# Where the block sums of w_down are taken: GpSimd or VectorE, one set behind each column tile of the output projection

## The chip, the cores and the metric

The kernel is one program on one core of a Trainium2 chip. The metric is the device time of one execution in microseconds; of several executions the median is given. The engines are named as the profile names them: PE (TensorE: matmuls and their weight loads), DVE (VectorE), ACT (ScalarE), POOL (GpSimd) and SP (SyncE, which here only issues DMAs). Each engine works its own queue in order; a semaphore holds an instruction, and all that stand behind it on that engine, until what it needs is there.

## The reference, cut to what matters

One decoder layer on 1032 tokens (1024 of a prompt, 8 of samples), width 1024, all float32:

```
proj = rmsnorm(x, norm1_w) @ w_in                       # SSD heads, gate and pooling inputs
y    = concat(ssd_heads(proj), pooled_groups(proj))     # 2048 columns: 12 tiles SSD, 4 tiles pooled
x    = x + y @ w_out                                    # the output projection
u    = causal_dwconv(rmsnorm(x, norm2_w) @ w_up)        # 2 x 2816 columns
gate, val = split(u, 2)
x    = x + (silu(gate) * val) @ w_down                  # 2816 -> 1024
out  = rmsnorm(x, final_norm_w)                         # and the new states
```

## The kernel before

Activations lie transposed: 128 channels on the partitions, 1032 tokens along a row. Every matmul is made of three in a faster number format, with each operand split in a high and a low part (`mm3`, L159 to L161: high by high, high by low, low by high). The high part is a copy on ACT, the low part a subtraction on DVE: L140 and L141 for weights (`raw` from memory to `wop`), L210 and L211 for activations.

The last matmul, by `w_down`, is done as a 2 by 2 block product with seven products in place of eight. Four of the seven (p5, p6, p7, p3) use sums of blocks of `w_down` as weights. These sums do not depend on any activation, so they are made long before they are used, beside the output projection, and stored to memory (`sd` tensors), from where the down phase loads them from 1126.7 us on (L1288).

The output projection (`w_out`, L907 on) runs over K in three passes: `part(ops, 0, 0)` with the first 6 SSD tiles, `part(ops, 6, 1)` with the other 6, and `w_out_end` with the 4 pooled tiles. Below, A0 to A7 are the 8 column tiles of the first pass and B0 to B7 those of the second. A tile is 3 chunks of 344 tokens with 18 matmuls each. For each tile SP loads two pieces of weights of 128x384 (four `raw` buffers: two tiles ahead), ACT and DVE split them (four `wop` buffers, so the pieces of tile n+2 are split when tile n has left theirs), PE multiplies, and DVE adds each chunk's bank to the residual `x` (the evacuation, L920). Four PSUM banks (tag `g`) take turns, so a chunk's bank is wanted again when three more chunks have run. The eighth tile of each pass runs its three chunks together (`gemm_k`).

Before the second pass, the six operands y of that pass are split (`yh` on ACT, `yl` on DVE, L210 and L211); the first of them was split early, the five others stand on the queues behind the last tile's weights.

There are twelve sets of sums, each one a pair (m, s) of a column block and a K piece. In the first pass sets 1 to 6 are made at tiles A0 to A5, in the second sets 7 to 12 at B1 to B6 (`first <= n < first + 6`). A set loads four blocks from `w_down` (`blk` "21" and "22" into one buffer, "11" and "12" into another), 256 KB each in sets 1 to 8 and 192 KB in the others, makes four sums (p5 = 21+22 into the place of 22, p7 = 11-21 into 21, p6 = 22-11 into a third buffer, p3 = 12-p6 into 12), and issues a store of each from POOL. The buffers are those that the pooling stage has left: the pair 11/12 has two buffers of the tag `v`, the pair 21/22 alternates between two tags, and so does the third. So the loads of a set wait until the stores of the set before last have landed. The loads stand on SP's queue among those of `w_out`.

A scheduler that replays the program in its own model of time sets the final order of each engine's queue; `issue_after` (here `self.behind`) keeps an instruction from being placed before another one.

Of the kernel before, what the change touches and what calls it, by code (L numbers as in the profile page):

```python
# [13 lines left out]
ALU = mybir.AluOpType  # L14
# [61 lines left out]
class Kernel:  # L76
# [817 lines left out]
    def w_out(self, pf):  # L894
        nc, d = self.nc, self.d
        ops = []
        for i in range(6):
            o = (self.bigt(F32R, TOK, "yh"), self.bigt(F32R, TOK, "yl"))
            self.split(self.xs[i][:, :TOK], *o)
            ops.append(o)  # L900
        self.x2 = []
        for n in range(KT):
            t = self.bigt(F32, TOK, "x2")
            nc.sync.dma_start(t, d["xT"][:, n])
            self.x2.append(t)

        self.sums = {}  # L907
        todo = [(m, s) for s in range(len(PIECES)) for m in range(KT // 2)]

        def part(ops, k0, first, done=None):  # L910
            for n in range(KT):
                if first <= n < first + 6:
                    self.down_sums(len(todo), *todo.pop(0))
                nk = len(ops)
                ws = self.load_tile(d["wout"][n][:, k0 * P : (k0 + nk) * P], nk, 3 if nk == 6 else 4)
                t = self.x2[n]

                def evac(c, ps):
                    tc_ = t[:, c * CH : (c + 1) * CH]
                    nc.vector.tensor_tensor(out=tc_, in0=tc_, in1=ps, op=ALU.add)  # L920

                (self.gemm_k if n == KT - 1 else self.gemm)(ws, ops, evac)
                if done is not None:
                    done(n)

        part(ops, 0, 0)
        ops = []
        for i in range(6, 12):
            o = (self.bigt(F32R, TOK, "yh"), self.bigt(F32R, TOK, "yl"))
            self.split(self.xs[i][:, :TOK], *o)  # L930
            ops.append(o)
        part(ops, 6, 1)
        ops = []
        for g in range(4):
            o = (self.bigt(F32R, TOK, "ph"), self.bigt(F32R, TOK, "pl"))
            self.split(pf[g], *o)
            ops.append(o)
        self.x2d = self.dram.tile([KT, P, TOK], F32, name="x2d")
        self.w_out_end(ops, 0)

        half = KT // 2
        self.ops = {p: [] for p in CHAIN}

        def beside(n):
            if n == 0:
                return
            for k in {1: (0, 1), 2: (2, 3), 5: (4, 5), 6: (6, 7)}.get(n, ()):
                self.scale(k, 0)
            for k in {3: (0, 1), 4: (2, 3), 6: (4, 5), 7: (6, 7)}.get(n, ()):
                t = self.op_tile()  # L950
                self.split(self.x2[k][:, :TH], t[:, 0], t[:, 1])
                self.ops["p1" if k < half else "p2"].append((t[:, 0], t[:, 1]))

        self.w_out_end(ops, 1, beside)
# [284 lines left out]

    def down_sums(self, i, m, s):  # L1240

        nc, d = self.nc, self.d
        k0, nk = PIECES[s]
        w = nk * P
        mk = lambda tag, bufs=1: self.ph.tile([P, 2, 512], F32, tag=tag, name=self.nm("ds"), bufs=bufs)
        x, y, z = mk("v", 2), mk(("mh", "ml")[i % 2]), mk(("sa", "sb")[i % 2])
        blk = {"11": x[:, 0, :w], "12": x[:, 1, :w], "21": y[:, 0, :w], "22": y[:, 1, :w]}
        for k, r, e in (("21", 1, 0), ("22", 1, 1), ("11", 0, 0), ("12", 0, 1)):
            o = (e * DK + k0) * P
            nc.sync.dma_start(blk[k], d["wdn"][2 * m + r][:, o : o + w])  # L1250

        def mix(p, out, in0, in1, op):
            nc.gpsimd.tensor_tensor(out=out, in0=in0, in1=in1, op=op)
            self.sums[p, m, s] = self.dram.tile([P, w], F32, name=self.nm("sd"))
            nc.gpsimd.dma_start(self.sums[p, m, s], out)

        s2 = z[:, 0, :w]
        mix("p5", blk["22"], blk["21"], blk["22"], ALU.add)
        mix("p7", blk["21"], blk["11"], blk["21"], ALU.subtract)
        mix("p6", s2, blk["22"], blk["11"], ALU.subtract)  # L1260
        mix("p3", blk["12"], blk["12"], s2, ALU.subtract)

    def down_ops(self, p, first=0, end=DK):

# [348 lines left out]
```

## Time and profile before

| what | value |
|---|---|
| median of 3 runs | 1409.85 us (1405.99 to 1411.67) |
| the profiled execution | 1407.76 us, span 1406.0 us |
| busy over the span | PE 97%, DVE 70%, ACT 50%, POOL 40% |
| PE clock granted, mean | 0.984 |
| DMA moved | 228.09 MB, 162 GB/s |
| the sums' stretch (L1250 to L1255) | first loads 507.0 us, first sum 533.5 us, last store issued 651.4 us |

The profile is one execution on the hardware. Times in it are microseconds from the start of the span. A busy PE is not yet a PE at its peak: matmuls overlap, and the granted clock is a column of its own (1.00 is full speed). A row of groups reads: line, engine, operation, out<-in, count, busy time and mean, then the idle time ahead of the group and what ended it. A row of the timeline reads: start, length, engine, line and operation, and in brackets the idle time ahead of it with its releaser. A row of waits reads: who waited for whom, total time, times, longest.

### The profile page before, as it was taken

To read this page: it belongs to the slowest core of one execution; us is meant where nothing else is said; L and a number is where in the kernel's file an instruction comes from. 1 tells how busy PE (TensorE), PEld (TensorE's weight loads), DVE (VectorE), ACT (ScalarE), POOL (GpSimd) and SP (SyncE) were. 2 spreads that over 40 slices of the span, in tenths; PEclk is the share of its full clock that TensorE was granted. 3 is DMA by queue.
4 is the path that set the end of the run, shared out by engine and by line. 5 is a ranking of instruction groups with operands and counts; after the bars stand their busy time and mean duration, and the time that the engine had idled before them with its cause. 6 is when DMAs were issued, how large, how long until landed. Compare 5 with 4: busy or idle time off the path is not lost. (4 is left out here: it accounts for less than half of the span.)

```text
span 1406.0 us, 26779 instructions
## 1 busy us (share of the span) xinstructions
PE 1360.4 (97%) x10360; PEld 1312.9 (93%) x10360; DVE 991.2 (70%) x1453; ACT 700.6 (50%) x1408; POOL 561.5 (40%) x704
## 2 busy tenths in 40 slices
PE   8999999979999999999979999999999999999997
PEld 7799879968799999899979999999999999999997
DVE  6575898669865684844689877777776787567743
ACT  6346774546644451311456545554554465444452
POOL 4233465888668305774222212212222224214122
PEclk9999999989999999999999999999999999999999
DMA  6031235243331256675477877777777769657513
GB/s 248 1 108 38 93 118 168 81 142 116 94 104 62 74 192 209 214 253 178 152 204 148 210 205 193 187 207 183 185 187 201 196 207 328 225 185 235 180 55 121
DMA packets 117820, 228.09 MB, mean 162 GB/s; under 512 B 19884, under 2 KB 37116, under 8 KB 117692
## 3 DMA queue, kind: packets, MB, share of 16 engines
q1 hardware_dynamic: 73772, 130.21, 29.3%
q0 software_dynamic: 27056, 70.22, 19.8%
q10 hardware_dynamic: 16864, 25.95, 5.6%
q8 instruction: 81, 1.33, 0.4%
q14 instruction: 47, 0.39, 0.1%
HBM read 169.64 MB, written 45.15 MB: 153 GB/s over the span
## 5 line engine op out<-in xcount | busy, mean ns | idle before, releaser
L1118 PE MATMUL g<-op,wop 128*128 128x258 f32 x3696 | 446.9, 283 | 4.3 <-DVE op L1048 1.6
L1118 PEld LDWEIGHTS g<-op,wop 128*128 128x128 f32 x3696 | 445.3, 189 | 5.6 <-DVE op L1048 2.0
L140 ACT ACTIVATE wop<-raw 128x512 fp32r<-128x512 f32 (+1 forms) x208 | 125.9, 608 | 231.2 <-PE g L161 139.7
L1300 PE MATMUL g<-op,wop 128*128 128x258 f32 x1848 | 224.9, 283 | 1.6 <-ACT op L210 0.9
L159 PE MATMUL g<-hh,wop 128*128 128x344 f32 x696 | 226.1, 325 | 0.0
L160 PE MATMUL g<-hl,wop 128*128 128x344 f32 x696 | 225.3, 324 | 0.0
L1300 PEld LDWEIGHTS g<-op,wop 128*128 128x128 f32 x1848 | 222.5, 189 | 2.7 <-ACT op L210 1.1
L161 PE MATMUL g<-hh,wop 128*128 128x344 f32 x696 | 224.8, 323 | 0.0
L141 DVE TENSOR_TENSOR wop<-raw,wop 128x512 fp32r<-128x512 f32 (+1 forms) x186 | 159.7, 862 | 83.3 <-ACT wop L140 81.5
L140 ACT ACTIVATE wop<-s 128x512 fp32r<-128x512 f32 (+1 forms) x136 | 83.6, 620 | 137.6 <-PE g L1300 51.9
L1098 POOL DMA_DIRECT2D s<-s x44 | 37.7, 857 | 249.8 <-DVE wop L141 89.2
L159 PEld LDWEIGHTS g<-hh,wop 128*128 128x128 f32 x696 | 132.2, 190 | 1.2 <-issue 1.1
L161 PEld LDWEIGHTS g<-hh,wop 128*128 128x128 f32 x696 | 132.1, 190 | 1.2 <-issue 1.2
L160 PEld LDWEIGHTS g<-hl,wop 128*128 128x128 f32 x696 | 132.1, 190 | 0.5 <-issue 0.4
L1200 DVE SCALAR_TENSOR_TENSOR acc<-u,cst,acc 128x1048 f32<-128x1048 f32 x88 | 115.2, 1309 | 12.2 <-ACT acc L1198 10.6
L141 DVE TENSOR_TENSOR wop<-s,wop 128x512 fp32r<-128x512 f32 (+1 forms) x136 | 92.1, 682 | 36.5 <-ACT wop L140 34.1
L1178 DVE TENSOR_TENSOR u<-u,g 128x258 f32<-128x258 f32 (+2 forms) x176 | 58.0, 354 | 72.2 <-PE g L1118 67.6
L1175 ACT ACTIVATE u<-g 128x258 f32<-128x258 f32 (+2 forms) x220 | 69.6, 340 | 71.2 <-PE g L1118 71.2
L160 PE MATMUL g<-yl,wop 128*128 128x344 f32 x288 | 93.4, 325 | 3.2 <-DVE yl L211 3.2
L161 PE MATMUL g<-yh,wop 128*128 128x344 f32 x288 | 93.0, 323 | 0.0
L159 PE MATMUL g<-yh,wop 128*128 128x344 f32 x288 | 92.9, 323 | 0.0
L1270 POOL DMA_DIRECT2D g<-td x77 | 41.2, 539 | 123.1 <-DVE op L211 70.2
(276 smaller groups left out, 2333.9 us busy)
## 6 DMA issues: line engine op xcount, KB each, us to landing
s<-wup SPq DMA_DIRECT2D x88, 256.0 KB, 3.2
g<-td POOLq DMA_DIRECT2D x77, 258.0 KB, 4.5
raw<-wup SPq DMA_DIRECT2D x66, 256.0 KB, 4.1
raw<-win SPq DMA_DIRECT2D x58, 256.0 KB, 2.7
mix<-acd SPq DMA_DIRECT2D x16, 768.0 KB, 4.5
td<-acc ACTq DMA_DIRECT2D x22, 516.0 KB, 6.1
s<-wup POOLq DMA_DIRECT2D x44, 256.0 KB, 5.3
s<-s POOLq DMA_DIRECT2D x44, 256.0 KB, 3.9
```

The source lines that it names most:

```text
L140: self.nc.scalar.activation(hi, raw[:, :w], AF.Copy)
L141: lo_eng.tensor_tensor(out=lo, in0=raw[:, :w], in1=hi.bitcast(F32), op=ALU.subtract)
L159: nc.tensor.matmul(ps[:, :n], wh, xh[:, sl], start=(first and k == 0), stop=False)
L160: nc.tensor.matmul(ps[:, :n], wh, xl[:, sl], start=False, stop=False)
L161: nc.tensor.matmul(ps[:, :n], wl, xh[:, sl], start=False, stop=(final and k == last))
L1098: nc.gpsimd.dma_start(t, raw[acc] if acc in raw else w[acc][j], accum_op=ALU.add)
L1118: nc.tensor.matmul(out, a, b, start=(p in OPENS and j == 1), stop=(j == 12), skip_group_check=True)
L1175: a = nc.scalar.activation(out, ps[:, s], AF.Copy, scale=-1.0 if p in ("p5", "p4") else 1.0)
L1178: nc.vector.tensor_tensor(out=out, in0=out, in1=ps[:, s], op=op)
L1200: nc.vector.scalar_tensor_tensor(out=acc, in0=u[:, k : k + FW], scalar=self.c("fw", 3 * n + k), in1=acc, op0=ALU.mult, op1=ALU.add)
L1270: self.loaded = self.nc.gpsimd.dma_start(st[:, j], self.td[i + j][ROW[p]]).ins
L1300: self.pe = nc.tensor.matmul(out, a, b, start=(s == 0 and i == 0 and j == 0), stop=(s == len(PIECES) - 1 and i == nk - 1 and j == 2),).ins
```

## The change

The four sums of a set are issued by DVE in place of POOL. The loads stay where they were, at the start of the set's tile; the sums are put behind that tile's last evacuation (`self.added` is the last L920 of the tile; `self.behind` keeps the sums from being placed ahead of it). The stores stay on POOL, each behind its sum. The arithmetic is the same.

```diff
         def part(ops, k0, first, done=None):
             for n in range(KT):
-                if first <= n < first + 6:
-                    self.down_sums(len(todo), *todo.pop(0))
+                add_up = self.down_sums(len(todo), *todo.pop(0)) if first <= n < first + 6 else None
...
                 def evac(c, ps):
                     tc_ = t[:, c * CH : (c + 1) * CH]
-                    nc.vector.tensor_tensor(out=tc_, in0=tc_, in1=ps, op=ALU.add)
+                    self.added = nc.vector.tensor_tensor(out=tc_, in0=tc_, in1=ps, op=ALU.add).ins
 
                 (self.gemm_k if n == KT - 1 else self.gemm)(ws, ops, evac)
+                if add_up is not None:
+                    with self.behind(self.added):
+                        add_up()
...
         def mix(p, out, in0, in1, op):
-            nc.gpsimd.tensor_tensor(out=out, in0=in0, in1=in1, op=op)
+            nc.vector.tensor_tensor(out=out, in0=in0, in1=in1, op=op)
             self.sums[p, m, s] = self.dram.tile([P, w], F32, name=self.nm("sd"))
             nc.gpsimd.dma_start(self.sums[p, m, s], out)
 
         s2 = z[:, 0, :w]
-        mix("p5", blk["22"], blk["21"], blk["22"], ALU.add)
-        mix("p7", blk["21"], blk["11"], blk["21"], ALU.subtract)
-        mix("p6", s2, blk["22"], blk["11"], ALU.subtract)
-        mix("p3", blk["12"], blk["12"], s2, ALU.subtract)
+
+        def add_up():
+            mix("p5", blk["22"], blk["21"], blk["22"], ALU.add)
+            mix("p7", blk["21"], blk["11"], blk["21"], ALU.subtract)
+            mix("p6", s2, blk["22"], blk["11"], ALU.subtract)
+            mix("p3", blk["12"], blk["12"], s2, ALU.subtract)
+
+        return add_up
```

On PE's and ACT's queues nothing moves. On POOL's the 48 sums are gone and the 48 stores follow each other. In the changed kernel the numbers of the lines are other: the evacuation is L919, the loads are L1253, the sums L1256 and the stores L1258.

DVE's queue where the first sums stand, beside tiles A1 to A3 (`x_5312` is the residual of A1, `x_5314` of A2; the `wop` named is that of the tile two later, in two pieces). Before:

```order
L141 TENSOR_TENSOR wop_5614<-raw_5612,wop_5614 128x384
L920 TENSOR_TENSOR x_5312<-x_5312,g_5484 128x344
L141 TENSOR_TENSOR wop_5619<-raw_5617,wop_5619 128x384
L920 TENSOR_TENSOR x_5314<-x_5314,g_5533 128x344
L920 TENSOR_TENSOR x_5314<-x_5314,g_5553 128x344
```

and now:

```order
L141 TENSOR_TENSOR wop_5607<-raw_5605,wop_5607 128x384
L1256 TENSOR_TENSOR ds_5327<-ds_5327 128x512
L1256 TENSOR_TENSOR ds_5416<-ds_5416 128x512
L1256 TENSOR_TENSOR ds_5327<-ds_5326,ds_5327 128x512
L1256 TENSOR_TENSOR ds_5328<-ds_5327,ds_5326 128x512
L1256 TENSOR_TENSOR ds_5416<-ds_5415,ds_5416 128x512
L1256 TENSOR_TENSOR ds_5417<-ds_5416,ds_5415 128x512
L919 TENSOR_TENSOR x_5314<-x_5314,g_5521 128x344
L1256 TENSOR_TENSOR ds_5326<-ds_5326,ds_5328 128x512
L1256 TENSOR_TENSOR ds_5415<-ds_5415,ds_5417 128x512
L919 TENSOR_TENSOR x_5314<-x_5314,g_5541 128x344
```

Sets 1 (`ds_5326` to `ds_5328`) and 2 (`ds_5415` to `ds_5417`) stand together behind the weights of A3 and around the first two evacuations of A2.

DVE's queue from the third chunk of A5 to the splits of the second pass's operands (`x_5320` is A5, `x_5322` A6; `wop_5932` and `wop_5937` belong to A7, `wop_6026` and `wop_6031` to B0). Before:

```order
L920 TENSOR_TENSOR x_5320<-x_5320,g_5840 128x344
L141 TENSOR_TENSOR wop_5937<-raw_5935,wop_5937 128x384
L920 TENSOR_TENSOR x_5322<-x_5322,g_5870 128x344
L920 TENSOR_TENSOR x_5322<-x_5322,g_5890 128x344
L141 TENSOR_TENSOR wop_6026<-raw_6024,wop_6026 128x384
L920 TENSOR_TENSOR x_5322<-x_5322,g_5910 128x344
L141 TENSOR_TENSOR wop_6031<-raw_6029,wop_6031 128x384
L211 TENSOR_TENSOR yl_6005<-xs_2087,yh_6004 128x1032
```

and now:

```order
L919 TENSOR_TENSOR x_5320<-x_5320,g_5828 128x344
L1256 TENSOR_TENSOR ds_5772<-ds_5772 128x512
L141 TENSOR_TENSOR wop_5937<-raw_5935,wop_5937 128x384
L1256 TENSOR_TENSOR ds_5772<-ds_5771,ds_5772 128x512
L1256 TENSOR_TENSOR ds_5773<-ds_5772,ds_5771 128x512
L919 TENSOR_TENSOR x_5322<-x_5322,g_5870 128x344
L1256 TENSOR_TENSOR ds_5771<-ds_5771,ds_5773 128x512
L919 TENSOR_TENSOR x_5322<-x_5322,g_5890 128x344
L141 TENSOR_TENSOR wop_6026<-raw_6024,wop_6026 128x384
L919 TENSOR_TENSOR x_5322<-x_5322,g_5910 128x344
L141 TENSOR_TENSOR wop_6031<-raw_6029,wop_6031 128x384
L211 TENSOR_TENSOR yl_6005<-xs_2087,yh_6004 128x1032
```

Set 6, the last of the first pass, stands ahead of B0's weights and of the splits; set 5 (`ds_5682`, `ds_5683`) stands just ahead of what is shown. No sum stands between the splits.

SP's queue over the loads of sets 5 and 6 (`ds_5683` and `ds_5682` are the pairs 21/22 and 11/12 of set 5, `ds_5772` and `ds_5771` those of set 6; `raw_5930` and `raw_5935` are A7's, `raw_6024` and `raw_6029` B0's weights). Before:

```order
L130 DMA raw_5935<-wout 128x384
L1250 DMA ds_5504<-wdn 128x512 x2
L1250 DMA ds_5593<-wdn 128x512 x2
L130 DMA raw_6024<-wout 128x384
L130 DMA raw_6029<-wout 128x384
L1250 DMA ds_5683<-wdn 128x512 x2
L130 DMA raw_6113<-wout 128x384
L130 DMA raw_6118<-wout 128x384
L1250 DMA ds_5772<-wdn 128x512 x2
L1250 DMA ds_5682<-wdn 128x512 x2
```

and now:

```order
L130 DMA raw_5930<-wout 128x384
L130 DMA raw_5935<-wout 128x384
L1253 DMA ds_5683<-wdn 128x512 x2
L1253 DMA ds_5772<-wdn 128x512 x2
L130 DMA raw_6024<-wout 128x384
L130 DMA raw_6029<-wout 128x384
L1253 DMA ds_5682<-wdn 128x512 x2
L1253 DMA ds_5771<-wdn 128x512 x2
L130 DMA raw_6101<-wout 128x384
```

The loads of set 5's second pair now stand behind both pieces of B0's weights, and those wait for a `raw` buffer, that is for DVE's splits of A6's weights. In the second pass the loads of set 9 stand behind the weights of B3, B4 and B5.

## The prediction

> **What bounds the kernel now.** I read the page's busy shares first, then who PE waited for, then the stretch of the sums in slices.
>
> ```profile
> PE 1360.4 (97%) x10360; PEld 1312.9 (93%) x10360; DVE 991.2 (70%) x1453; ACT 700.6 (50%) x1408; POOL 561.5 (40%) x704
> PE g L160 <- DVE yl L211: 3.2, 2, 2.8
> 520.00:560.00 40.00, 40.00 (x256) 40.00 (x255) 18.60 (x27) 8.24 (x15) 17.80 (x20) 1.00 0.72 236
> 560.00:600.00 40.00, 36.82 (x216) 36.09 (x215) 34.70 (x27) 12.03 (x16) 29.81 (x30) 0.91 0.69 221
> 600.00:640.00 40.00, 40.00 (x256) 40.00 (x255) 17.35 (x27) 4.74 (x9) 29.91 (x36) 1.00 0.76 248
> ```
>
> (The slices give length, then busy time of PE, PEld, DVE, ACT and POOL, then PE's granted clock, DMA share and GB/s.) PE sets the time. Where PE is full at clock 1.00, nothing that leaves DVE or POOL shortens the kernel. In the whole stretch of the sums PE loses time in one place, between 560 and 600: 3.2 us in two waits, both for `yl`, the splits of the second pass's operands. A finer cut shows a second loss behind the first:
>
> ```profile
> 586.00:588.00 2.00, 1.40 (x9) 1.12 (x8) 2.00 (x1) 0.00 (x0) 2.00 (x3) 1.00 0.52 197
> 588.00:590.00 2.00, 0.00 (x0) 0.00 (x0) 2.00 (x1) 0.00 (x0) 2.00 (x3) 0.91 0.00 0
> 590.00:592.00 2.00, 1.41 (x4) 0.97 (x5) 2.00 (x4) 1.82 (x3) 0.09 (x1) 0.50 0.78 279
> 592.00:594.00 2.00, 2.00 (x8) 2.00 (x9) 2.00 (x4) 1.57 (x2) 0.00 (x0) 0.50 0.96 241
> 594.00:596.00 2.00, 2.00 (x9) 2.00 (x9) 2.00 (x4) 0.00 (x0) 0.74 (x1) 0.50 0.27 102
> ```
>
> After the gap PE runs at half clock for some 6 us. What both cost together is read from ACT's splits of weights, the second of which starts when PE has finished a tile:
>
> ```profile
> 568.44 0.53 ACT L140 ACTIVATE wop<-raw 128x384 fp32r<-128x384 f32 x1 [0.89 <-PE g L161]
> 576.94 0.53 ACT L140 ACTIVATE wop<-raw 128x384 fp32r<-128x384 f32 x1 [0.89 <-PE g L161]
> ...
> 608.72 0.53 ACT L140 ACTIVATE wop<-raw 128x384 fp32r<-128x384 f32 x1 [0.90 <-PE g L161]
> ```
>
> A tile takes 8.50 us (576.94 - 568.44). A6 ends at 576.94 and B1 at 608.72; the three tiles A7, B0 and B1 should take 25.5 us and took 31.78. **The loss is 6.3 us**, 3.2 waiting and 3.1 at half clock.
>
> Why the splits were late:
>
> ```profile
> 511.84 3.51 DVE L211 TENSOR_TENSOR yl<-xs,yh 128x1032 fp32r<-128x1032 f32 x3
> ...
> 560.51 6.20 DVE L141 TENSOR_TENSOR wop<-raw,wop 128x384 fp32r<-128x384 f32 x1
> ...
> 577.49 0.56 DVE L141 TENSOR_TENSOR wop<-raw,wop 128x384 fp32r<-128x384 f32 x1
> 578.19 11.96 DVE L211 TENSOR_TENSOR yl<-xs,yh 128x1032 fp32r<-128x1032 f32 x4
> 590.07 0.55 DVE L141 TENSOR_TENSOR wop<-raw,wop 128x384 fp32r<-128x384 f32 x1
> 590.54 1.22 DVE L211 TENSOR_TENSOR yl<-xs,yh 128x1032 fp32r<-128x1032 f32 x1
> ```
>
> ```profile
> 560.46 5.03 POOL L1253 TENSOR_TENSOR ds<-ds,ds 128x512 f32<-128x512 f32 x4
> ...
> 579.17 4.54 POOL L1253 TENSOR_TENSOR ds<-ds,ds 128x512 f32<-128x512 f32 x2
> 583.65 1.63 POOL L1255 DMA_DIRECT2D sd<-ds  x3
> 585.30 3.75 POOL L1253 TENSOR_TENSOR ds<-ds,ds 128x512 f32<-128x512 f32 x3
> ```
>
> Three splits take 3.51 us when POOL has no sums, 1.17 each; four take 11.96 while POOL sums, 7.3 us over the 4.7 they need. A subtraction that takes 0.55 alone takes 6.20 across four sums of POOL in a row. So POOL's sums hold DVE up.
>
> **What the change removes and adds.** POOL loses its 48 sums:
>
> ```profile
> L1253 POOL TENSOR_TENSOR ds<-ds,ds 128x512 f32<-128x512 f32 (+1 forms) x36 | 45.7, 1287 | 6.9 <-DMA ds<-wdn 6.6
> L1253 POOL TENSOR_TENSOR ds<-ds 128x512 f32<-128x512 f32 (+1 forms) x12 | 15.3, 1278 | 39.6 <-DMA ds<-wdn 39.6
> L1237 DVE TENSOR_TENSOR acc<-acc,acc 128x516 f32<-128x516 f32 x11 | 7.6, 688 | 0.0
> ```
>
> 61.0 us off POOL cost PE nothing by themselves. On DVE, where no sum ran before, the nearest rows bound one: 0.69 us for 128x516 with both operands in SBUF (L1237) and 0.55 for 128x384 (L141 above); from below nothing is faster, from above a sum that waits for the one before it may cost its whole 0.69 rather than the 0.6 at which independent ones follow each other. I take 0.65 and 0.55: 32 x 0.65 + 16 x 0.55 = 29.6 us. A tile's share is 4 x 0.65 = 2.6, beside three evacuations (0.5 each) and two splits (0.55): 5.2 of 8.5 us. DVE has the room; this lies under PE. What matters is the order: a sum that waits for its blocks now stops the evacuations and splits behind it.
>
> **The path to the splits, step by step.** The waits are those of the buffers, with these durations:
>
> ```profile
> 528.50 1.75 SPq L1250 DMA_DIRECT2D ds<-wdn  x4
> ...
> 533.46 2.86 POOL L1253 TENSOR_TENSOR ds<-ds 128x512 f32<-128x512 f32 x2 [14.00 <-DMA ds<-wdn]
> ...
> ds<-wdn SPq DMA_DIRECT2D x12, 256.0 KB, 4.2
> sd<-ds POOLq DMA_DIRECT2D x10, 256.0 KB, 3.8
> ...
> L1255 POOL DMA_DIRECT2D sd<-ds x48: 540/557/603, 536.3 to 651.4; - x48
> ...
> DMA to landing us min/median/max: 2.2/3.2/6.1
> ...
> L1250 SPq DMA_DIRECT2D ds<-wdn x48: 327/422/632, 507.0 to 643.5; - x48
> ...
> DMA to landing us min/median/max: 2.2/3.6/6.5
> ```
>
> (The two landing rows are of the stores `sd` and of the loads `ds`, over all 48.) Sets 1 and 2 are in at 533.46 and wait behind A3's weights, done at 535.6 (A1 ends at 534.45, five tiles ahead of A6; plus 0.53 on ACT and 0.55 on DVE). Eight sums and two evacuations end near 541.8. Set 1's p7 is done at 537.5, its store is issued by 538.1 and lands at 541.9; SP issues set 3's first pair, 0.42 apart, the second of it in at 546.5. p5 of set 3 is up at 544.0, behind A4's second split, and waits 2.5 us; A3's first evacuation behind it is due at 545.8, and its bank is wanted 8.5 us later. The round trip from p7 to the next load is 9 us, of 17 that two tiles allow. Set 3's p7 then waits for A3's last evacuation, A5's first split and set 4's p5, and ends at 553.2; its store lands at 557.6, set 5's first pair at 562.2. p5 of set 5 waits some 2 us for it, A6's second split behind it ends at 563.4, frees the `raw` buffer of B0's weights, and only then SP reaches set 5's second pair: the block that p7 needs is issued at 564.1 and in at 568.3. Seven sums, two splits and two evacuations on, DVE is through both sets at 574.9, evacuates A6, splits B0's weights (ACT is ready at 577.47) and reaches the five `yl` at 578.0, as before (578.19). Four at 1.2, with ACT's `yh` (1.07 each) between, end at 583.1, then B1's split, then the fifth at 584.8. When PE wants them:
>
> ```profile
> 587.08 0.32 PE L159 MATMUL g<-yh,wop 128*128 128x344 f32 x1
> 590.21 0.66 PE L160 MATMUL g<-yl,wop 128*128 128x344 f32 x1 [2.80 <-DVE yl L211]
> ```
>
> The fourth at 587.2, where it stopped, the fifth three matmuls on, at 587.7. **Slack 2.9 us, so the wait goes, and the half clock with it: -6.3 us.** The splits' cover is what this slack is; with it gone each late microsecond is one of PE.
>
> In the second pass each set has a tile to itself, and the same round trip fits. The last store is out near 648 on a chain with less in it than before (651.4), well ahead of what takes its buffers. The 700 to 760 us stretch, where PE loses more, keeps its order on all engines; nothing is gained or lost there.
>
> [...]
>
> **The sum.** 1407.76 of the profiled execution (span 1406.0, 1.8 around it) less 6.3 is 1401.5. The median of the runs is 2.1 above that execution: 1409.85 - 6.3 = **1403.6 us**, 0.45% less.
>
> **Rivals.**
> - *Half the gain.* The drop to half clock need not follow every such gap.
>
> ```profile
> 712.00:714.00 2.00, 0.00 (x0) 0.00 (x0) 2.00 (x5) 1.44 (x9) 0.00 (x0) 0.63 0.14 32
> ...
> 730.00:732.00 2.00, 0.76 (x5) 0.36 (x3) 2.00 (x5) 1.15 (x2) 0.85 (x1) 1.00 1.05 242
> ```
>
> For it: a gap of 1.2 us (730 to 732) left the clock at 1.00, and the runs before spread over 5.7 us. Against it: the gap of 3 us was followed by it here, and so was one of over 2 us at 712. If the median run before did not pay it, only the 3.2 us of waiting go: 1406.7. [...]
> - *The splits stay late.* Loads landing 3 to 6 us later than their medians at set 5 would use up the slack; the gap stays in part. 1406.5 to 1410. For it: the hand-made chain has two round trips in a row. Against: a mean DMA share of 0.72.
> - *Slower.* The place is p7 of set 5. With all landings at their maximum (store 6.1, load 6.5 where I took 3.8 and 4.2) the two round trips take 4.6 us more each, 9.2 together. A7's first split, behind that p7 and due at 570.1, would come at 579.3, and A7 starts at 576.94: a first gap of 3 us with its own half clock (3.1), then the rest of 9.2 - 2.9 = 6.3 us of waiting at B0 with the old half clock. 6.3 + 6.2 against 6.3 now: +6.2, 1416. It is slower than now from 6.1 us of lateness on.
> - *Nothing changes* since ACT's `yh`, not POOL, sets the splits. Against: ACT waits for DVE there, not the other way, and 511.84 shows the pair at full pace.
>
> ```profile
> 582.58 1.07 ACT L210 ACTIVATE yh<-xs 128x1032 fp32r<-128x1032 f32 x1 [1.91 <-DVE yl L211]
> ```
>
> That gives 1409.9; it is counted with the late splits.
>
> **Chances.** Full gain 0.62; half 0.15; splits late or nothing 0.13; slower 0.10. Range 1399 to 1411.5: the full gain with the runs' own spread below, the second and third case above; what it leaves out is the slow case and the tails. A measurement of this kernel tells about 0.5% from no change, 7.0 us: faster is below 1402.8, slower above 1416.9. The forecast lies 0.8 us inside "no change"; of the full gain somewhat under half should come out below the line (0.29), with 0.04 from gains that I do not see. Faster 0.33, same 0.58, slower 0.09.
>
> **What would show it.** No wait of PE for `yl`; clock 1.00 and 65 matmuls in each 10 us from 520 to 700; B1 ending 25.5 us after A6; `yl` at 1.23 each; no POOL sums; DVE's sums at 0.55 to 0.69. Wrong would be: sums of DVE waiting long for `ds<-wdn`, PE waiting for a `wop` split or a bank between 535 and 655, or `yl` still starting late.

## The result, and the profile after

The changed kernel took **1397.0 us** (median of five executions, 1395.76 to 1399.9); the kernel before, timed five times in all by then, 1406.56 us. The ratio is 0.9935 with a 95% interval of 0.9907 to 0.9963: 0.65% faster, above the 0.5% that the prediction calls distinguishable. The forecast of 1403.6 us is 6.6 us too high, and 1397.0 lies 2.0 us below its range.

The page of the changed kernel, its busy time, and then the stretch of the sums in the same slices as before (length, busy time of PE, PEld, DVE, ACT and POOL, PE's clock, DMA share, GB/s):

```profile
PE 1359.6 (97%) x10360; PEld 1312.8 (94%) x10360; DVE 986.9 (71%) x1501; ACT 701.3 (50%) x1408; POOL 496.8 (36%) x656
```

```profile
520.00:560.00 40.00, 40.00 (x257) 40.00 (x256) 22.66 (x41) 7.64 (x14) 8.69 (x16) 1.00 0.87 294
560.00:600.00 40.00, 40.00 (x256) 40.00 (x255) 27.05 (x41) 12.60 (x17) 4.30 (x8) 1.00 0.58 193
600.00:640.00 40.00, 40.00 (x256) 40.00 (x255) 22.26 (x44) 4.73 (x9) 10.76 (x20) 1.00 0.73 238
```

PE is full at clock 1.00 in all three; the slice that had 36.82 us of work at 0.91 now has 40.00 at 1.00, and no wait of PE for `yl` is left. ACT's second splits of weights, which start when PE has finished a tile, give the length of A7, B0 and B1:

```profile
574.78 0.53 ACT L140 ACTIVATE wop<-raw 128x384 fp32r<-128x384 f32 x1 [0.89 <-PE g L161]
...
600.26 0.53 ACT L140 ACTIVATE wop<-raw 128x384 fp32r<-128x384 f32 x1 [0.90 <-PE g L161]
```

600.26 - 574.78 = 25.48 us, against 31.78 before: **6.30 us gained at the border of the passes**, the 6.3 of the forecast. But A6 already ends 2.16 us earlier than in the profile of before (576.94), and what follows B1 is 0.56 us longer (1398.1 - 600.26 = 797.84 against 1406.0 - 608.72 = 797.28). The spans differ by 7.9 us: 6.30 + 2.16 - 0.56. The 2.16 us are not of the change: in all 18 profiles of this document a split of weights on ACT (L140) starts 76.90 us ahead of A6's end, at 500.04 us before and 497.88 now, when no block of `w_down` has been loaded yet (507.0 and 504.9).

DVE's queue at the waits for blocks, and at the splits:

```profile
544.26 0.69 DVE L1256 TENSOR_TENSOR ds<-ds 128x512 f32<-128x512 f32 x1 [2.33 <-DMA ds<-wdn]
560.95 0.69 DVE L1256 TENSOR_TENSOR ds<-ds 128x512 f32<-128x512 f32 x1 [2.64 <-DMA ds<-wdn]
567.09 1.29 DVE L1256 TENSOR_TENSOR ds<-ds,ds 128x512 f32<-128x512 f32 x2 [3.12 <-DMA ds<-wdn]
```

```profile
576.03 4.94 DVE L211 TENSOR_TENSOR yl<-xs,yh 128x1032 fp32r<-128x1032 f32 x4
...
581.36 1.23 DVE L211 TENSOR_TENSOR yl<-xs,yh 128x1032 fp32r<-128x1032 f32 x1
```

Four `yl` take 4.94 us where they took 11.96. The three waits are those that the prediction walks through: p5 of set 3, p5 and p7 of set 5. The sums themselves, from DVE's groups (count, busy time, mean ns, idle time ahead):

```profile
L1256 DVE TENSOR_TENSOR ds<-ds,ds 128x512 f32<-128x512 f32 (+1 forms) x36 | 21.9, 641 | 3.3 <-DMA ds<-wdn 3.1
L1256 DVE TENSOR_TENSOR ds<-ds 128x512 f32<-128x512 f32 (+1 forms) x12 | 7.6, 642 | 5.0 <-DMA ds<-wdn 5.0
```

29.5 us in all. DVE's busy total falls, from 991.2 to 986.9 us, but that fall lies outside this stretch. Over the stretch that holds all the sums, from 507 us before and 504.84 now to the same point of PE's work (935 matmuls), DVE is busy 2.0 us longer (third busy time):

```profile
507.00:660.00 153.00, 149.82 (x935) 149.09 (x934) 89.26 (x103) 39.32 (x64) 86.11 (x97) 0.98 0.69 226
504.84:651.54 146.70, 146.70 (x935) 146.70 (x934) 91.29 (x151) 39.32 (x64) 26.35 (x49) 1.00 0.71 236
```

So of the 29.5 us that DVE now spends on the sums, it had lost some 27 before to being held up by POOL's.

### The profile page after: what moved, and what is told of

Its sections match the earlier page's. It is cut to its first block, busy times and chain, and to the rows that moved or that the text cites. A ratio compares the mean times of both kernels' runs of the same rounds, so it can differ in the third digit from the quotient of the medians.

```text
span 1398.1 us, 26823 instructions
## 1 busy us (share of the span) xinstructions
PE 1359.6 (97%) x10360; PEld 1312.8 (94%) x10360; DVE 986.9 (71%) x1501; ACT 701.3 (50%) x1408; POOL 496.8 (36%) x656
## 4 chain that ended last, share of the span: by engine, by line
PE 82%; DVE 7%; DMA 3%; POOL 3%; issue 3%; ACT 2%; DVEq 0%; SPq 0%; POOLq 0%; ACTq 0%
PE g L1120 30%; PE g L1307 15%; PE g L160 10%; PE g L161 10%; PE g L159 10%; DVE wop L141 1%; DVE mix L583 1%; PE pY L620 1%; DVE xd L578 1%; POOL st L680 1%; DMA s<-wup 1%; DVE xs L516 1%; DVE xs L638 1%; PE pY L630 1%; DVE mix L538 1%
## 5 line engine op out<-in xcount | busy, mean ns | idle before, releaser
L140 ACT ACTIVATE wop<-raw 128x512 fp32r<-128x512 f32 (+1 forms) x208 | 125.9, 608 | 228.1 <-PE g L161 134.3
L141 DVE TENSOR_TENSOR wop<-raw,wop 128x512 fp32r<-128x512 f32 (+1 forms) x186 | 139.2, 752 | 88.6 <-ACT wop L140 86.6
L140 ACT ACTIVATE wop<-s 128x512 fp32r<-128x512 f32 (+1 forms) x136 | 83.6, 620 | 140.2 <-PE g L1307 51.9
```

The costliest lines, as they stand in the source:

```text
L140: self.nc.scalar.activation(hi, raw[:, :w], AF.Copy)
L141: lo_eng.tensor_tensor(out=lo, in0=raw[:, :w], in1=hi.bitcast(F32), op=ALU.subtract)
```

## The experiments

Every profile is cut below in three: the *head* up to A6's end, the *border* A7 to B1, and the *tail* from B1's end to the end of the span, each read from the same ACT rows as above. A kernel timed in several rounds has its median and its ratio to the kernel before, which was timed beside it. The kernel before had medians of 1404.78 to 1408.6 us in these groups.

| kernel | head | border | tail | median, ratio to before |
|---|---|---|---|---|
| before | 576.94 | 31.78 | 797.28 | |
| before, again | 586.38 | 31.38 | 796.34 | |
| changed | 574.78 | 25.48 | 797.84 | 1397.0, 0.9935 (0.9907 to 0.9963) |
| changed, 2nd | 577.67 | 25.48 | 797.05 | 1401.71, 0.9964 (0.9938 to 0.9990) |
| changed, 3rd | 569.13 | 25.48 | 796.99 | 1401.82, 0.9946 (0.9924 to 0.9968) |
| no sums | 573.04 | 25.47 | 796.99 | 1398.97, 0.9934 (0.9906 to 0.9963) |
| first pass on DVE only | 576.53 | 31.77 | 797.40 | 1402.96, 0.9970 (0.9943 to 0.9998) |
| second pass on DVE only | 579.07 | 33.53 | 797.10 | 1405.79, 0.9994 (0.9969 to 1.0019) |
| sums on DVE, not kept behind | 582.11 | 29.92 | 795.57 | 1403.09, 0.9960 (0.9935 to 0.9985) |
| changed + 3 adds on POOL | 571.31 | 26.00 | 797.09 | |
| changed + 5 adds on POOL | 576.13 | 27.09 | 797.38 | |
| changed + 3 stores, 3 adds | 574.86 | 26.03 | 797.31 | |
| changed + 5 adds, 4 of blocks | 577.31 | 27.15 | 797.14 | |
| the same + 3 stores | 587.36 | 26.06 | 797.28 | |
| changed + 4 sums in real form | 577.76 | 26.45 | 796.99 | |
| changed + one `ce` on DVE | 579.33 | 25.48 | 797.79 | 1403.62, 0.9969 (0.9945 to 0.9994) |
| changed + `ssq` on DVE | 574.19 | 25.48 | 794.13 | 1394.93, 0.9900 (0.9877 to 0.9922) |
| the same, again | 580.89 | 25.48 | 795.53 | 1399.75, 0.9960 (0.9936 to 0.9985) |

### Is the gain 6 us or 9?

The changed kernel, twice more.

> The changed kernel itself once more, timed in alternation with the kernel before. Theory 1 (the gain is the one stall at the border of the two passes, 6.3 us, and the rest of the 9.6 us seen so far is scatter between executions): 5 to 8 us less than before, ratio 0.9943 to 0.9964. Theory 2 (there is a second gain of some 3 us, for example in the 700 to 760 us stretch or ahead of the sums): 8.5 to 11 us less, ratio 0.9922 to 0.9940. In both the tiles A7, B0 and B1 together take 25.5 us.

> The changed kernel a third time, beside the next three. By ten profiles so far the time from B1's end to the last instruction is 796.3 to 797.8 us in all of them, the three tiles A7 to B1 take 25.5 us in the changed kernel and 31.4 to 31.8 us in the kernel before, and the time up to A6's end lies anywhere from 571.3 to 577.9 us in kernels that have the same order up to there (586.4 less one tile). If that is all (theory 1): 5 to 8 us less than before, ratio 0.9943 to 0.9964, and the two intervals so far, 0.9907 to 0.9963 and 0.9938 to 0.9990, both hold it. Theory 2 (a gain of 9 us or more): ratio below 0.9938.

1401.71 (12 executions) and 1401.82 us (10): 4.5 and 6.8 us less than before, the first a little under the 5 to 8 us of theory 1. Weighted by their intervals the three ratios average 0.9949, which is 7.2 us, give or take 0.0014 or 2 us if the intervals are taken at their word; 6.3 us lies in all three. By the times alone the low end of theory 2 is not excluded, but no profile shows a second gain, so theory 2 is not needed. The two longer series ran on two chips, each with the kernel before beside it; what the chip adds to the scatter is open. (The second text takes 577.9 for A6's end in the second profile of before; the row is 586.38, the head differs by still more.)

The table says where the scatter is. The border is 25.48 us in every profile of the changed kernel, the tail is 796.3 to 797.8 us with any placing of the sums that leaves the order behind them alone; the head runs from 569 to 587 us. PE's waits in one of the longest heads and in the shortest, the second profile of before and the third of the changed kernel (who waited for whom, total, times, longest):

```profile
PE pY L630 <- POOL ce L553: 9.5, 2, 9.1
PE pM L597 <- DVE xd L578: 7.0, 2, 6.8
PE pM L565 <- DVE h L610: 7.0, 4, 4.5
```

```profile
PE pY L630 <- POOL ce L553: 5.0, 2, 4.5
PE pM L565 <- DVE h L610: 3.2, 4, 1.9
PE pM L597 <- DVE xd L578: 0.3, 1, 0.3
```

4.5 + 6.7 + 3.8 = 15.0 of the 17.25 us between these heads. All three waits lie in the SSD stage, 150 us and more ahead of the sums.

### The sums left out

In the kernel before:

```diff
         def mix(p, out, in0, in1, op):
-            nc.gpsimd.tensor_tensor(out=out, in0=in0, in1=in1, op=op)
             self.sums[p, m, s] = self.dram.tile([P, w], F32, name=self.nm("sd"))
...
```

(The rest of this change lets p6 be stored from the buffer of block 11, so the third buffer of a set falls away too.)

> The kernel before with its 48 sums left out: the blocks are loaded and stored as they are, so the down phase multiplies by unsummed blocks. DVE has no more to do than before and POOL nothing but stores. Theory 1 (only POOL's hold on DVE cost time, and the 29.5 us of sums on DVE are free): as fast as the changed kernel, 5 to 8 us less than before; A7 to B1 in 25.5 us. Rival (the sums on DVE cost something of their own that eats part of the gain): faster than the changed kernel by 1 us or more.

The border is 25.47 us, as in the changed kernel, and the tail the same. The median is 2.7 us below that of the changed kernel beside it, which would speak for the rival; but neither stretch in which the sums could cost anything shows it, and the heads differ by 4.6 us. By the profiles the 29.5 us of sums cost nothing on DVE, and the change has taken all that the sums could give.

### Half of the change

```diff
-            nc.vector.tensor_tensor(out=out, in0=in0, in1=in1, op=op)
+            (nc.vector if i > 6 else nc.gpsimd).tensor_tensor(out=out, in0=in0, in1=in1, op=op)
...
-        return add_up
+        if i > 6:
+            return add_up
+        add_up()
```

(and with `i <= 6` for the other half; i counts down from 12, so i > 6 are the sets of the first pass).

> Only the six sets of the first pass are summed on DVE behind the tile, the six of the second pass on POOL as before. Theory 1 (the only place that cost time is the border, where POOL ran sums of sets 5 and 6 beside the splits yl): the whole gain, 5 to 8 us less than before, A7 to B1 in 25.5 us. Rival (POOL's sums cost something in the second pass too): 2 us or more slower than the changed kernel.

> The other half alone: sets 7 to 12 on DVE, sets 1 to 6 on POOL as before. Theory 1: the stall at the border stays, four yl take about 12 us, PE waits some 3 us for yl and falls to half clock: within 2 us of before; A7 to B1 in 30 to 33 us. Rival (POOL's load in the whole stretch counts, not the overlap at the border): half the gain, 3 us less.

With sets 7 to 12 alone on DVE the stall stays: `yl` takes 12.10 us, PE waits 5.5 us for it, and the border is 33.53.

```profile
580.33 12.10 DVE L211 TENSOR_TENSOR yl<-xs,yh 128x1032 fp32r<-128x1032 f32 x4
```

```profile
PE g L160 <- DVE yl L211: 5.5, 2, 2.9
```

With sets 1 to 6 alone I expected the whole gain, and the profile says 31.77 us: none of it, in that execution. DVE and POOL there:

```profile
587.95 3.26 DVE L211 TENSOR_TENSOR pl<-pf,ph 128x1032 fp32r<-128x1032 f32 x1
...
591.98 3.78 DVE L211 TENSOR_TENSOR pl<-pf,ph 128x1032 fp32r<-128x1032 f32 x1
```

```profile
588.82 1.29 POOL L1256 TENSOR_TENSOR ds<-ds 128x512 f32<-128x512 f32 x1
590.05 1.09 POOL L1258 DMA_DIRECT2D sd<-ds  x2
591.16 2.54 POOL L1256 TENSOR_TENSOR ds<-ds,ds 128x512 f32<-128x512 f32 x2
593.65 1.02 POOL L1256 TENSOR_TENSOR ds<-ds 128x384 f32<-128x384 f32 x1
```

and PE, which waits 3.9 us in all between A6's and B1's end (2.7 for evacuations, 1.0 for a split of weights, 0.2 for `yl`), with its longest wait and the slice behind it (its clock is the third number from the end):

```profile
601.06 0.65 PE L159 MATMUL g<-yh,wop 128*128 128x344 f32 x1 [2.21 <-DVE x L919]
```

```profile
602.00:604.00 2.00, 2.00 (x8) 2.00 (x8) 2.00 (x6) 0.00 (x0) 0.00 (x0) 0.53 0.00 0
```

Since DVE finishes set 6 early, the blocks of sets 7 to 9 come early too, and POOL sums them from 581 to 599 (in the kernel before the first of them ran at 595), beside the splits `yl` and `pl` again (`pl` are the splits of the pooled operands). The stall moved 10 us on, to the next things that DVE owes PE. Whether this happens in every execution is open: the median, 1402.96, lies 4.5 us below the profiled execution, and its interval reaches from next to none of the gain to more than all of it.

### The place of the sums on DVE

The sums on DVE, with nothing that keeps them behind the tile's evacuation:

```diff
-                if add_up is not None:
-                    with self.behind(self.added):
-                        add_up()
...
-        return add_up
+        add_up()
```

> The sums on DVE, but not kept behind the tile's last evacuation: they stand on DVE's queue where the scheduler puts them, and so two of them between the splits yl, where one waits for its blocks. Theory (a sum that waits for blocks holds all behind it on DVE, so the place is as much of the change as the engine): PE waits for yl again, A7 to B1 in 29 to 36 us, the kernel 3 us or more slower than the changed one. Rival (POOL's hold was all, the place doesn't matter): within 2 us of the changed kernel, A7 to B1 in 25.5 us.

```profile
583.69 0.69 DVE L1253 TENSOR_TENSOR ds<-ds 128x512 f32<-128x512 f32 x1 [3.90 <-DMA ds<-wdn]
...
588.62 1.23 DVE L211 TENSOR_TENSOR yl<-xs,yh 128x1032 fp32r<-128x1032 f32 x1
589.76 0.68 DVE L1253 TENSOR_TENSOR ds<-ds 128x512 f32<-128x512 f32 x1
590.36 2.37 DVE L211 TENSOR_TENSOR yl<-xs,yh 128x1032 fp32r<-128x1032 f32 x2
...
595.60 0.42 PE L160 MATMUL g<-yl,wop 128*128 128x344 f32 x1 [2.08 <-DVE yl L211]
```

Here a sum waits 3.90 us for its blocks ahead of B0's weights, and sums stand between the splits. PE waits 2.3 us and the border is 29.92: 4.4 of the 6.3 us are lost again, though every split takes its 1.23 us. The scheduler orders the feed-forward stage a little otherwise here too, whose tail is 1.4 us shorter; the median is 1.3 us above that of the changed kernel timed beside it. The place shows at the border; by the medians alone it could not be told.

### How POOL holds DVE

Adds on POOL beside `yl` in the changed kernel, with nothing else moved on PE, ACT and DVE (three and five of them):

```diff
             ops.append(o)
+            if i == 7:
+                for _ in range(3):
+                    nc.gpsimd.tensor_tensor(out=self.free, in0=o[1][:, :512], in1=o[1][:, 512:1024], op=ALU.add)
...
-        s2 = z[:, 0, :w]
+        s2, self.free = z[:, 0, :w], z[:, 1]
```

> The changed kernel with three additional adds of 128x512 on POOL, which wait for the first of the late yl and so run beside the next ones; their result goes to an unused half of a buffer. The orders of PE, ACT, DVE and SP are those of the changed kernel. Theory (POOL's sums hold DVE up by their own length, 1.3 us each): yl later by some 4 us, of which 2.9 us is slack; PE waits 1 us or a little more, the clock stays at 1.00, A7 to B1 takes 26 to 27.5 us. Rival (something else made the splits late, for example ACT's yh): 25.5 us.

> The same with five such adds, as many as POOL had there in the kernel before. Theory: yl later by 6.5 us or more, PE waits about 3.5 us and then runs at half clock for some 6 us; A7 to B1 takes 30 to 33 us, the whole loss of the kernel before. Rival: 25.5 us.

```profile
577.38 7.07 DVE L211 TENSOR_TENSOR yl<-xs,yh 128x1032 fp32r<-128x1032 f32 x4
```

```profile
578.79 10.63 POOL L936 TENSOR_TENSOR ds<-yl 128x512 f32<-128x512 f32 x5 [4.43 <-DVE yl L211]
...
588.32 0.42 PE L160 MATMUL g<-yl,wop 128*128 128x344 f32 x1 [1.25 <-DVE yl L211]
```

Direction right, size not: three adds cost 0.5 us at the border (the least of the 0.5 to 2 forecast) and five 1.6, with a wait of PE of 1.25 us and the clock at 1.00, where I expected 4.5 to 7.5 us. The two engines took turns: each add 2.1 to 2.3 us in place of 1.3, each split up to 2.33 in place of 1.23. In the second profile of the kernel before, three real sums ran through and one split of weights (0.55 us alone) was held for the whole of them:

```profile
595.55 4.75 DVE L141 TENSOR_TENSOR wop<-raw,wop 128x384 fp32r<-128x384 f32 x1
```

```profile
594.48 1.63 POOL L1255 DMA_DIRECT2D sd<-ds  x3
596.13 3.74 POOL L1253 TENSOR_TENSOR ds<-ds,ds 128x512 f32<-128x512 f32 x3
```

It is the same in all three profiles with sets 5 and 6 on POOL: two sums in turns (some 4.5 us), three stores, then three sums at 1.25 us each and one operation of DVE held 4.75 us or more. Neither sets 5 and 6 nor three stores are needed for it: in the profile with the first pass on DVE, shown above, three sums of sets 8 and 9 behind two stores (591.16 to 594.67) ran through beside one `pl` of 3.78 us. So I tried stores ahead, adds that read the block buffers, both, and the four real sums of set 6 made a second time in place:

> The kernel with three additional adds on POOL beside yl once more, with three additional stores of a yl (256 KB each) issued by POOL just ahead of them. In the kernel before, three sums right behind three stores took 1.25 us each and one split beside them 5.42 us; the three or five additional adds alone took 2.1 to 2.3 us each, in turns with the splits. Theory A (behind stores POOL's adds run through and hold DVE for all of their time): the adds take 1.3 us each, one split beside them 4.5 us or more. Theory B (the additional adds take turns with DVE in any case, and something else made the difference): 2.1 us or more each, no split over 2.4 us.

> The changed kernel with one additional add on POOL that reads yl (it sets the time) and behind it four that read the block buffers, in the form of the real sums (two inputs of 128x512 from two buffers, output into a third). Theory C (it is what the adds read: with inputs away from yl POOL runs through at 1.25 us each and DVE gets no turn): the four adds take about 5 us together, one split beside them 5 us or more, PE waits for yl and A7 to B1 takes 28 to 32 us. Theory B (adds take turns with DVE whatever they read): 2 us or more each, no split over 2.4 us, A7 to B1 26 to 27 us.

> The same with three additional stores issued by POOL ahead of the adds. Theory D (both are needed, stores ahead and block buffers read): only here, and not without the stores, the four adds take 1.25 us each and one split 5 us or more. Theory B: in turns here too, 2 us or more each.

> The changed kernel in which POOL makes the four sums of set 6 a second time, in place on the same buffers, once their stores have landed (some 577 us, beside the splits yl); the results are not stored. Theory E (the form or the start of the real sums lets POOL run through): the four take about 5 us, one split beside them 4.5 us or more, A7 to B1 28 us or more. Theory B (adds take turns with DVE here too): 2 us or more each, no split over 2.4 us, and the long hold in the kernel before stays unexplained.

In all four POOL and DVE took turns: the adds 1.8 to 2.1 us each on the mean, no split over 2.34 us, border 26.03, 27.15, 26.06 and 26.45 us. Theories A, C, D and E fall; theory B has the turns right, and its figures (2 or 2.1 us or more for an add, a border of 26 to 27 us) to within 0.3 us. **What lets POOL run through is open.** The lengths fit turns: an add of 1.3 us and a split of 1.2 come to 2.5, and each took up to 2.1 to 2.3 us beside the other. A hold across three back-to-back sums (3.74 us of POOL, 4.75 us of DVE above) does not fit them, and no run shows where it comes from.

### The kernel before, a second time

> The kernel before itself, profiled a second time. If the loss at the border is the same in every execution: A7 to B1 in 31 to 33 us again, with PE waiting some 3 us for yl and a clock of 0.50 behind it. If the drop of the clock is left to chance (the rival of half the gain): a wait of 3 us without it, 28.7 us. The part ahead of A6's end, which the change doesn't touch, may differ from 576.9 us by several us; the part behind B1's end should again take 797 us.

```profile
601.50 0.66 PE L160 MATMUL g<-yl,wop 128*128 128x344 f32 x1 [4.17 <-DVE yl L211]
602.00:604.00 2.00, 2.00 (x9) 2.00 (x8) 2.00 (x4) 0.54 (x1) 0.00 (x0) 0.50 1.02 301
```

A wait of 4.17 us, then a clock of 0.50; border 31.38. The loss is 5.9 us here and was 6.3 in the first profile, split otherwise between waiting (4.2 against 3.2) and clock (1.7 against 3.1).

That the clock dropped both times does not make it certain in every execution. All 18 profiles have the same gap of 2.28 us near 16 us, ahead of everything that differs between them. In twelve the clock falls to 0.50 behind it, in six it stays at 1.00; here the first profile of before and the third of the changed kernel:

```profile
16.00:18.00 2.00, 2.00 (x8) 1.85 (x9) 2.00 (x4) 0.54 (x2) 0.64 (x1) 0.55 1.06 376
```

```profile
16.00:18.00 2.00, 1.45 (x7) 1.16 (x8) 2.00 (x4) 0.49 (x1) 0.92 (x1) 1.00 1.06 375
```

Between 10 and 1400 us of the 18 profiles, all 36 gaps of PE of 3.2 us or more were followed by a clock of 0.50; of the 67 between 2 and 3.2 us 53 were and 14 were not, one of 3.18 us among these. At the border the waits of 2.08 to 4.17 us, in five profiles, all were. In how many executions the kernel before pays the second half of its loss is therefore not known.

### Two more holds of POOL

The profile pointed to two more places where POOL stands in PE's way. One product `ce` of the SSD stage waits on POOL's queue behind steps of the sample tiles (the ends of the two lines are left out here):

```diff
-            nc.gpsimd.tensor_tensor(out=ce, in0=ce, in1=cc...
+            (nc.vector if q == c == 1 else nc.gpsimd).tensor_tensor(out=ce, in0=ce, in1=cc...
```

> The changed kernel with one more product moved from POOL to DVE: of the 14 products ce of the SSD phase the one of the second head group's chunk 1, which stands on POOL's queue behind steps of the sample tiles that wait for their own loads. In six profiles PE waited there for ce 9.1 us three times and 4.6 us three times, before and after alike, which is the largest difference between executions. Theory 3 (the scatter of some 4.5 us and a fixed loss of 4.6 us come from that place on POOL's queue): no wait over 2 us there, 4 to 8 us less than the changed kernel, 10 to 14 less than before, ratio to before 0.990 to 0.993. Rival (the next thing is as late, for example h on POOL or the mix of the same chunk): within 2 us of the changed kernel, ratio 0.994 to 0.997.

```profile
PE pM L565 <- DVE h L610: 14.3, 6, 9.2
```

The wait for `ce` falls to 0.4 us, but one for `h`, 9.2 us at its longest, takes its place, and the head is 579.33. The rival is right: 1403.62 us, no gain.

The other is the second half of the pooled pass, where POOL adds the sums of squares (L983):

```diff
-                    nc.gpsimd.tensor_tensor(out=ssq, in0=ssq, in1=sq, op=ALU.add)
+                    (nc.vector if t else nc.gpsimd).tensor_tensor(out=ssq, in0=ssq, in1=sq, op=ALU.add)
```

> The changed kernel with the five sums of squares of the second half of the pooled pass on DVE in place of POOL, where each of 1.5 to 1.7 us ran beside DVE's splits (one split of 0.68 us took 1.79). Theory (POOL's hold on DVE costs PE there too): the waits of PE for sq, 2.7 and 1.6 us, get shorter by 1 us or so, and the time from B1's end to the end of the span is 795 to 796.5 us in place of 797.1. Rival (DVE is full there, 10.00 of 10 us between 690 and 700, and the five adds of 0.69 us cost as much as they free): 797 us or more.

> The kernel with the sums of squares on DVE once more. Its profile showed 794.1 us from B1's end to the end of the span, 2.9 us less than the changed kernel (797.0 to 797.8 in three profiles). Theory (the gain is this 2.9 us and 6.3 us at the border, the rest of the first measurement was luck ahead of the sums): 7 to 11 us less than before, ratio 0.992 to 0.995, tail 793.5 to 795 us. Rival (more than that, as the first time): ratio under 0.991.

A split of weights beside the pooled pass, first in the changed kernel and then in this one:

```profile
688.00 1.79 DVE L141 TENSOR_TENSOR wop<-raw,wop 128x512 fp32r<-128x512 f32 x1
```

```profile
696.29 0.69 DVE L141 TENSOR_TENSOR wop<-raw,wop 128x512 fp32r<-128x512 f32 x1
```

and PE's waits for the squares, in the same order:

```profile
PE pM L986 <- ACT sq L978: 4.3, 2, 2.7
```

```profile
PE pM L986 <- ACT sq L978: 2.8, 1, 2.8
```

The tail is 794.13 and 795.53 us in two profiles, 1.5 to 3.7 us less than the changed kernel's 796.99 to 797.84; each time it missed the forecast of the theory, by 0.9 us on the short side and then by 0.5 us on the long one. The second ratio, 0.9960, lies above the 0.992 to 0.995 of the theory, and the rival wanted less than 0.991. The two ratios, 0.9900 and 0.9960, average 0.9927, but the two intervals do not meet, though it is one kernel: a series scatters by more than its interval says. With that in mind, it beats both kernels by the profiles' tail, and by the times at least the kernel before; against the changed kernel the times alone do not settle 2 us.

## Why the prediction was right or wrong, point by point

- **What bounds the kernel, and where it loses: right.** The gain at the border is 6.30 us in the pair of profiles, and leaving the sums out gives the same 25.47 us.
- **Cost of a sum on DVE: right.** 29.5 us against 29.6, and nothing of it on the path.
- **The path to the splits: right to a microsecond.** p5 of set 3 waits 2.33 us (2.5 forecast), p5 of set 5 2.64 (some 2), and p7 of set 5 runs at 567.09, 1.0 us later than forecast once the head's 2.16 us are taken off. DVE reaches `yl` at 576.03 (575.8 by the same shift), and the fifth is done at 582.59 (582.6). PE, 2.16 us earlier as well, wants it at 585.5: the slack of 2.9 us is there. The stores took POOL 540 to 586 ns each beside DVE's sums, no longer than the 540 to 603 ns of before, so it was right that the forecast has no term for them.
- **Half clock goes with the wait: right in both profiles of before, but not shown for every execution.** The waits of 2.08 to 4.17 us at the border were followed by a clock of 0.50, at a price of 1.7 to 3.1 us, those of 1.25 and 1.28 us were not. But the same gap of 2.28 us near 16 us kept the clock at 1.00 in six of 18 profiles, so the doubt behind the rival *half the gain* was sound. That rival did not come about in the profiles; for the executions that were only timed it stays open, since 3.2 us and 6.3 us differ by less than the medians scatter. That -6.3 held for the pair of profiles is in part luck.
- ***The splits stay late* and *nothing changes*: fell for this change**, and the first is what happens without the place behind the evacuation (29.92). *Slower* never came near: the median landings between 500 and 580 us were 4.9 us for loads and 4.3 for stores, a little above the 4.2 and 3.8 taken and far from its 6.5 and 6.1.
- **The sum is the step that failed.** It ends with "1409.85 - 6.3": the -6.3 held in the profiles, the level did not. 1409.85 was a median of three executions, with an offset of 2.1 us added to the profiled one to reach it; longer series of the same kernel have medians of 1404.8 to 1408.6. Without the offset the sum stood at 1401.5, and the changed kernel's longer series have 1401.7 and 1401.8; that it comes so near is in part luck, since 1407.76 was a single execution too. The first five, with 1397.0, lie 4.7 us under those. Of these only the slowest, 1399.9, has a profile, so where the others were faster is not shown; the changed kernel's heads, 569 to 578 us, scatter enough for it. I had read "the runs' own spread" from three values (5.7 us), took 1399 for the lower end from it, and did not ask which stretch spreads: the head alone moved by 18 us between the profiles here.
- **The chances:** same 0.58, faster 0.33. The change came out as faster the first time (0.65%), as 0.36% and 0.54% later. With a gain of 0.45%, next to the line of 0.5%, the two were close to even, and I leaned too far to one of them.
- **What POOL's sums do to DVE: right in place, not fully understood.** Taking POOL's sums away from the border freed it (25.48 and 25.47 us), leaving them there for either half of the sets brought the stall back in the profile (33.53 and 31.77 us); adds put there by hand bring back only 0.5 to 1.7 us.

## What to carry to other kernels

A gain of half a per cent was found here by cutting the span at landmarks on either side of the changed stretch and comparing the pieces: the stretch without a stall repeats to 0.01 us while the part ahead of it scatters by 18. A forecast should add its difference to a level that comes from many executions, and take its range from the scatter of the stretches that the change does not touch. When work of POOL that holds up DVE is moved in part, look where the rest of it will then run: here it came earlier (from 581 us on, not 595) and, in the one profile taken, held up what DVE did next (a `pl` took 3.26 and 3.78 us, and 1.22 without sums beside it).

## What the runs showed of the hardware that I had not expected

- POOL and DVE held each other up in two ways. With the adds put there by hand they took turns, an add and a split of some 2.1 to 2.3 us each; but in three profiles of three with sets 5 and 6 on POOL, three sums right behind three stores ran at 1.25 us each while one operation of DVE (0.55 or 1.17 us alone) was held for 4.75 us or more, and with sets 8 and 9 on POOL a shorter hold, 3.78 us, came behind two stores. Six kernels with adds put there did not reproduce the second.
- The price of the half clock was not one figure: 3.1 us behind a wait of 2.8 and 0.4 us, 1.7 behind one of 4.17, about 2.1 behind one of 2.08. Whether it is paid at all varied too: the same gap of 2.28 us was followed by it in twelve profiles of 18.
- The time up to A6's end was 569 to 587 us, and all of this scatter arises ahead of the first load of the sums' blocks, where the kernels (but the one with `ce` moved) do the same: between two of these profiles, 17 us apart, 15 us are three waits of the SSD stage.
